# Packed copies for the dilated scores, and a paired, fixed order of the attention loop

## The chip, the cores and the metric

One core of a Trainium2 chip runs the whole block in one launch. The metric is device time in microseconds (us), the median of several executions. The engines in the profile: PE is the matrix engine (TensorE), PEld its weight loads, DVE the vector engine, ACT the scalar engine, POOL GpSimd, SP the engine whose queue issues most DMAs.

## What is computed

The reference is a transformer block on 1024 tokens of width 1024: a modulated norm, an input projection, an mLSTM mixer and a dilated attention mixer side by side, an output projection, and an expert-choice feed-forward with 16 experts. The change touches the attention mixer alone:

```python
DILATED_PATTERNS = ((128, 1), (512, 4), (2048, 16))
def dilated_attention_mixer(a_q, a_k, a_v, q_norm_g, k_norm_g, rel_bias):
    q = rms_norm(heads(a_q), q_norm_g); k = rms_norm(heads(a_k), k_norm_g); v = heads(a_v)
    outs, lses = zip(*[dilated_window_attention(q, k, v, rel_bias, w, d) for w, d in DILATED_PATTERNS])
    weights = jax.nn.softmax(jnp.stack(lses), axis=0)
    return jnp.sum(weights[..., None] * jnp.stack(outs), axis=0)
```

In a pattern with dilation d a token attends to tokens of its own phase (position modulo d) in a window. There are 8 heads of 64 columns.

## The kernel before

The kernel runs in stages: input projection and mLSTM; `phase_attn` (381 to 560 us); `phase_out`, which multiplies with the output weights and prepares the routing (560 to 680 us); and `phase_experts` (680 us to the end).

`phase_attn` works in 64 units: 4 pairs of heads, in each pair first 8 units of `order` 0 (dilation 1) and then 8 of `order` 1 (dilations 4 and 16 joined in one table), the two heads of the pair in turn. One unit is two blocks of 128 queries against 256 keys:

- `attn_A` (L807 on): for each block two score matmuls into a PSUM tile `sp` (3 buffers), with the high part `kh` (L818) and the low part `kl` (L819) of the keys; then DVE adds a table and takes the minimum (L825), and ACT takes the exponential with its sum (L830).
- `attn_B`, two units later: four transposes of `p` on PE (L845), and a copy of the result to `pT` by DVE (L855) or ACT (L857).
- `attn_C`, for two units at once: 16 matmuls with the values (L876), and a DVE copy of the result, to `ya` in order 0 (L878) or with a step of 8 floats into `O2` in order 1 (L881).

q and k lie transposed in SBUF, tokens along the row (`qT`, `kh`, `kl`, 1024 floats each). Order 0 reads neighbouring tokens. Order 1 reads them through a view: the stationary q with a step of 8 floats (`q8`), the moving keys with a step of 16 floats (`kh4`, `kl4`), quoted below.

Beside the units run side streams, one step per unit: `attn_pair_norm` (norms of the next pair of heads), `attn_pair_T` (its transposes and its split into high and low parts), `attn_load_1` and `attn_load_2` (tables and values from DRAM; `attn_load_2` loads `t_raw` into a buffer that the squares of `attn_pair_norm` use too, and ACT turns it into the order-1 table `t2`, L741), `attn_merge` (joins the outputs of the two orders of a pair; its statistics and weights go through DRAM), and `mix_stream` (L1071 to L1079). The mix stream is the mLSTM half of the output projection: 16 units of 12 matmuls, one group of 3 per step, then an ACT copy to the single buffer `mx_ev`, a POOL DMA that adds x into it, and an SP store to `part_d`, which waits for that DMA. In the loop the mix stream is asked in 7 of 8 units (`MIX = 8`); what is left of it runs in `phase_out`, together with the first steps of the merge of the last pair.

Each engine runs its instructions in a fixed sequence. Where nothing else is said, a planner chooses that sequence from the program's order and its own estimate of readiness; instructions passed to `keep_in_program_order` keep the order in which the program names them.

```python
q8 = qT.rearrange("p (n u c) -> p c u n", u=2, c=4)
kh4 = kh.rearrange("p (a b c) -> p c b a", b=4, c=4)
...
    if order == 0:
        w0 = min(max(P * i - 64, 0), S - 256)
        ql, kwh, kwl = qT[:, i * P:(i + 1) * P], kh[:, w0:w0 + 256], kl[:, w0:w0 + 256]
    else:
        ql, kwh, kwl = q8[:, i // 2, i % 2], kh4[:, i // 2], kl4[:, i // 2]
```

Of the kernel before, what the change touches and what calls it, by code (L numbers as in the profile page):

```python
# [11 lines left out]
F32 = mybir.dt.float32  # L12
F32R = mybir.dt.float32r
# [7 lines left out]
P = 128  # L21
# [30 lines left out]
MIX = 8  # L52
# [54 lines left out]
class K:  # L107
# [11 lines left out]
    def fill(self, pool, n):  # L119

        self.nc.gpsimd.memset(pool.tile([P, n // 4], F32, name="fill"), 0.0)

# [638 lines left out]

    def attn_pair_T(self, hp, psum, pool):
# [4 lines left out]
        if hp < 2:  # L767

            self.kl[hp] = []
            for z in range(2):  # L770
                kl = pool.tile([P, S], F32R, name=f"kTl{z}")
                nc.gpsimd.memset(kl[AE * (1 - z):AE * (2 - z)].bitcast(F32), 0.0)
                self.kl[hp].append(kl)
        T = [(pool.tile([P, S], F32R, name="qT", bufs=2), pool.tile([P, S], F32R, name="kTh", bufs=2), self.kl[hp % 2][z]) for z in range(2)]
        self.pairs[hp]["T"] = T
        for b in range(2):
            t = slice(b * 512, (b + 1) * 512)
            for j in (1, 0):
                pf = psum()
                for i in range(4):  # L780
                    nc.tensor.transpose(pf[:, i * P:(i + 1) * P], qk[:, j, 4 * b + i, :], self.ident)
# [18 lines left out]
    def attn_A(self, u):  # L800
# [9 lines left out]
        u["p"] = pt = [aw.tile([P, 256], F32, name="p", bufs=6) for _ in range(2)]  # L810
        for j in range(2):
            i = 2 * g + j
            if order == 0:
                w0 = min(max(P * i - 64, 0), S - 256)
                ql, kwh, kwl = qT[:, i * P:(i + 1) * P], kh[:, w0:w0 + 256], kl[:, w0:w0 + 256]
# [3 lines left out]
            nc.tensor.matmul(sp[:, j, :], ql, kwl, start=False, stop=True)  # L819
# [12 lines left out]
    def attn_B(self, u):  # L832
# [4 lines left out]
        u["ts"] = ts = aw.tile([P, 2, 2, P], F32, name="pT", bufs=3)  # L837
        for j in range(2):
            for w in range(2):
# [5 lines left out]
                nc.tensor.transpose(tp[:a1 - a0, j, w, :], pt[j][:, a0:a1], self.ident)  # L845
# [13 lines left out]
    def attn_C(self, us):  # L859
# [5 lines left out]
        for j in range(2):  # L865
            i = 2 * g + j
            for w in range(2):
                for z in range(2):
# [7 lines left out]
                    nc.tensor.matmul(op[zs, j * P:(j + 1) * P], lv, us[z]["ts"][:kp, j, w, :], start=(w == 0), stop=(w == 1))  # L876
# [58 lines left out]
    def phase_attn(self, st):  # L935
# [15 lines left out]
        for s in range(n + 3):  # L951
            if s < n:
                u = units[s]
                if s % 16 == 0:
                    self.O2[s // 16] = self.m1.tile([P, S], F32, name="O2", tag="xTh", bufs=2)
                hp = s // 16
                if s % 16 == 4 and hp:
                    self.attn_load_2(hp)
                if s % 16 == 2 and hp < 3:
                    self.attn_pair_norm(hp + 1)  # L960
                if s % 16 == 8 and hp < 3:
                    side.append(self.attn_pair_T(hp + 1, psum, aw if hp % 2 == 0 else self.ta))
                if s % 16 == 13 and hp < 2:
                    self.attn_load_qk(hp + 2)
                if s % 16 == 12 and hp < 3:
                    self.attn_load_1(hp + 1)
                self.attn_A(u)
            if s == 48:
                side.append(self.ada_rows(aw, psum, 6, 8))
            if 0 <= s - 2 < n:  # L970
                self.attn_B(units[s - 2])
            if s >= 4 and s % 2 == 0:
                self.attn_C(units[s - 4:s - 2])
            if s >= 19 and (s - 19) % 16 == 0 and s < n:
                side.append(self.attn_merge((s - 19) // 16, psum))
# [771 lines left out]
```

## Time and profile before

| | us |
|---|---|
| median of 3 executions (1836.42 to 1842.91) | 1841.47 |
| the profiled execution | 1833.95 |
| its span, first to last instruction | 1832.0 |
| input projection, mLSTM, start | 0 to 381 |
| attention loop, first to last score | 381 to 554 |
| its end and the output projection's first three rows | 554 to 594 |
| rest of the output projection, routing | 594 to 680 |
| experts | 680 to 1832 |

The time of an execution is its span and about 2 us around it. A row of a group gives line, engine, operation, output<-inputs, shape, count, then the busy time in us and the mean of one in ns, then the idle time of the engine before it. A row of a timeline gives start, duration, engine, line, operation, tiles, shape and count; durations of matmuls overlap, so a matmul's price is the distance from its start to the next start.

### The profile page before, as it was taken

What the parts mean: (1) busy time and instruction counts of PE and PEld (TensorE: products, weight loads), DVE (VectorE), ACT (ScalarE), POOL (GpSimd) and SP (SyncE); (2) the same over time, 40 slices, a digit from 0 to 9 for tenths busy, and PEclk for the clock granted to TensorE, in tenths of its full rate; (3) what the DMA queues carried; (4) which work ended last, traced back from release to release, by engine and by line L of the source; (5) the groups of instructions that cost most, each with busy time, mean ns of one, the idle gap of its engine ahead of it and who ended that gap; (6) DMA issues with size and microseconds to landing.
All of it is one profiled execution on the core that took longest, in us unless ns stands there. A gap on an engine that the chain in (4) does not pass through costs nothing. (4 is left out here: it accounts for less than half of the span.)

```text
span 1832.0 us, 24429 instructions
## 1 busy us (share of the span) xinstructions
PE 1722.9 (94%) x8696; PEld 1402.8 (77%) x8696; DVE 1487.1 (81%) x2156; ACT 1197.7 (65%) x1603; POOL 180.5 (10%) x185
## 2 busy tenths in 40 slices
PE   5999999989998939999999999999999999999997
PEld 4777888778886827888888778777787777777785
DVE  5578885687866788988988898888898888888886
ACT  5346454377763537787777777776776776777764
POOL 1001000031123020010110000100000001001000
PEclk9999999999999959999999999999999999999999
DMA  9135663325557768999999999999999999999892
GB/s 325 42 114 172 213 215 98 110 80 116 135 129 227 258 255 336 359 354 382 410 363 345 373 345 379 372 335 390 352 369 384 357 364 387 329 382 368 311 391 67
DMA packets 152553, 517.26 MB, mean 282 GB/s; under 512 B 33163, under 2 KB 50833, under 8 KB 116721
## 3 DMA queue, kind: packets, MB, share of 16 engines
q1 hardware_dynamic: 138560, 478.92, 70.7%
q0 software_dynamic: 10960, 36.32, 7.5%
q8 instruction: 68, 1.11, 0.2%
q10 hardware_dynamic: 2912, 0.48, 0.2%
q14 instruction: 53, 0.43, 0.1%
HBM read 488.16 MB, written 27.50 MB: 281 GB/s over the span
## 5 line engine op out<-in xcount | busy, mean ns | idle before, releaser
L1505 DVE TENSOR_TENSOR wl<-w,wh 128x2048 fp32r<-128x2048 f32 x278 | 627.8, 2285 | 81.6 <-ACT wh L1489 81.2
L1489 ACT ACTIVATE wh<-w 128x2048 fp32r<-128x2048 f32 x278 | 523.1, 1919 | 55.2 <-PE py L1524 26.3
L1505 DVE TENSOR_TENSOR wl<-w_half,wh 128x1024 fp32r<-128x1024 f32 x210 | 245.6, 1217 | 8.6 <-ACT wh L1489 8.5
L1489 ACT ACTIVATE wh<-w_half 128x1024 fp32r<-128x1024 f32 x210 | 211.8, 1058 | 24.1 <-PE px L1524 13.1
L1524 PE MATMUL py<-wl,xTh 128*128 128x512 f32 x512 | 139.9, 394 | 7.7 <-DVE wl L1505 7.7
L1524 PE MATMUL px<-wl,xTh 128*128 128x512 f32 x512 | 139.7, 394 | 4.5 <-DVE wl L1505 4.5
L1524 PE MATMUL px<-wh,xTh 128*128 128x512 f32 x512 | 141.1, 395 | 2.3 <-ACT xTh L124 2.1
L1524 PE MATMUL py<-wh,xTh 128*128 128x512 f32 x512 | 140.8, 394 | 2.2 <-ACT wh L1489 2.0
L1524 PE MATMUL py<-wh,xTl 128*128 128x512 f32 x512 | 138.3, 390 | 0.0
L1524 PE MATMUL px<-wh,xTl 128*128 128x512 f32 x512 | 138.1, 391 | 0.0
L1524 PE MATMUL px<-wh,hT 128*128 128x512 f32 x512 | 130.4, 396 | 0.1
L1524 PE MATMUL py<-wh,hT 128*128 128x512 f32 x512 | 129.0, 393 | 0.0
L1524 PEld LDWEIGHTS py<-wl,xTh 128*128 128x128 f32 x512 | 94.6, 188 | 33.4 <-DVE wl L1505 14.6
L1524 PEld LDWEIGHTS px<-wl,xTh 128*128 128x128 f32 x512 | 95.0, 188 | 29.5 <-DVE wl L1505 10.4
L1524 PEld LDWEIGHTS px<-wh,xTh 128*128 128x128 f32 x512 | 95.3, 189 | 23.9 <-ACT xTh L124 2.5
L1524 PEld LDWEIGHTS py<-wh,xTh 128*128 128x128 f32 x512 | 94.7, 188 | 24.0 <-ACT wh L1489 4.5
L1524 PEld LDWEIGHTS px<-wh,hT 128*128 128x128 f32 x512 | 95.6, 190 | 22.1 <-ACT wh L1489 2.1
L1524 PEld LDWEIGHTS px<-wh,xTl 128*128 128x128 f32 x512 | 96.7, 189 | 20.6
L1524 PEld LDWEIGHTS py<-wh,xTl 128*128 128x128 f32 x512 | 96.0, 188 | 20.4 <-DVE xTl L125 0.2
L1524 PEld LDWEIGHTS py<-wh,hT 128*128 128x128 f32 x512 | 95.0, 188 | 20.8 <-ACT wh L1489 0.7
L1581 POOL DMA_INDIRECT out_dram<-xin,idx x16 | 48.3, 3019 | 590.6 <-DVE xin L1580 590.6
L1445 POOL DMA_INDIRECT xin<-h_d,idx x16 | 37.8, 2362 | 477.9 <-DVE rg L1443 197.4
(456 smaller groups left out, 3138.2 us busy)
## 6 DMA issues: line engine op xcount, KB each, us to landing
w<-in_w_down_dram SPq DMA_DIRECT2D x95, 1024.0 KB, 8.4
w<-in_w_gate_dram SPq DMA_DIRECT2D x91, 1024.0 KB, 7.2
w<-in_w_up_dram SPq DMA_DIRECT2D x88, 1024.0 KB, 7.1
w_half<-in_w_gate_dram SPq DMA_DIRECT2D x70, 512.0 KB, 7.6
w_half<-in_w_up_dram SPq DMA_DIRECT2D x70, 512.0 KB, 7.5
w_half<-in_w_down_dram SPq DMA_DIRECT2D x66, 512.0 KB, 8.3
ada_w<-in_w_ada_dram SPq DMA_DIRECT2D x64, 256.0 KB, 3.5
wraw<-in_w_in_dram SPq DMA_DIRECT2D x20, 512.0 KB, 4.3
```

The costliest lines, as they stand in the source:

```text
L1445: nc.gpsimd.indirect_dma_start(out=xin, out_offset=None, in_=self.h2_d, in_offset=bass.IndirectOffsetOnAxis(ap=idx[:, :1], axis=0))
L1489: act = self.nc.scalar.activation(h[:, j * m:(j + 1) * m], t, AF.Copy)
L1505: self.tc.keep_in_program_order(self.nc.vector.tensor_sub(l[:, c], t, h[:, c]))
L1524: nc.tensor.matmul(ps[c], x[:, t], y[:, o:o + 512], start=first and q == 0 and t == 0, stop=last and (q, t) == (2, FF // N - 1))
L1581: nc.gpsimd.indirect_dma_start(out=self.out, out_offset=bass.IndirectOffsetOnAxis(ap=u["idx"][:, :1], axis=0), in_=y, in_offset=None, comp ...
```

## The change

1. `attn_turn` is new. For each pair of heads it makes six packed copies: for each head q, `kh` and `kl` in the order (phase, token in the phase), so that the tokens of a phase lie side by side. Copies 0, 3 and 5 are made by DVE, 1, 2 and 4 by ACT. They are emitted in units 1 to 6 of a pair. Order 1 then reads the copies as order 0 reads its tiles, with no step.
2. The low parts `kl` exist once, no longer in two sets, and all tiles of `attn_pair_T` come from one pool.
3. The loop goes over pairs of units: the scores of two units, two steps of the mix stream (instead of 7 in 8 units), `attn_C` for the pair three rounds back (before: two), `attn_B` for the pair one round back, then two steps of each side stream. `p` has 8 buffers instead of 6, `pT` 6 instead of 3.
4. The PE instructions of scores, transposes, values and mix stream keep the program's order (`pin`).

```diff
-MIX = 8
+    def attn_turn(self, hp, j):
+        nc, (z, what) = self.nc, divmod(j, 3)
+        src = self.pairs[hp]["T"][z][what]
+        dst = self.aw.tile([P, S], F32R, name=("qP", "kPh", f"kPl{z}")[what], bufs=1 if what == 2 else 2)
+        if what == 0:
+            o, i = dst.rearrange("p (c u n) -> p c u n", c=4, u=2), src.rearrange("p (n u c) -> p c u n", u=2, c=4)
+        else:
+            o, i = dst.rearrange("p (c b a) -> p c b a", c=4, b=4), src.rearrange("p (a b c) -> p c b a", b=4, c=4)
+        if j in (0, 3, 5):
+            nc.vector.tensor_copy(o, i)
+        else:
+            nc.scalar.activation(o, i, AF.Copy)
+        self.pairs[hp].setdefault("turned", []).append(dst)
...
-        T = [(pool.tile([P, S], F32R, name="qT", bufs=2), pool.tile([P, S], F32R, name="kTh", bufs=2), self.kl[hp % 2][z]) for z in range(2)]
+        T = [(pool.tile([P, S], F32R, name="qT", bufs=2), pool.tile([P, S], F32R, name="kTh", bufs=2), self.kl[z]) for z in range(2)]
...
-        qT, kh, kl = pr["T"][h % 2]
-        q8 = qT.rearrange("p (n u c) -> p c u n", u=2, c=4)
-        kh4 = kh.rearrange("p (a b c) -> p c b a", b=4, c=4)
-        kl4 = kl.rearrange("p (a b c) -> p c b a", b=4, c=4)
+        qT, kh, kl = pr["turned"][3 * (h % 2):][:3] if order else pr["T"][h % 2]
...
-                ql, kwh, kwl = q8[:, i // 2, i % 2], kh4[:, i // 2], kl4[:, i // 2]
-            nc.tensor.matmul(sp[:, j, :], ql, kwh, start=True, stop=False)
+                w0 = i // 2 * 256
+            ql, kwh, kwl = qT[:, i * P:(i + 1) * P], kh[:, w0:w0 + 256], kl[:, w0:w0 + 256]
+            self.pin(nc.tensor.matmul(sp[:, j, :], ql, kwh, start=True, stop=False))
...
+        for s2 in range(0, n + 6, 2):
+            for s in (s2, s2 + 1):
+                if s < n:
...
+                        side.append(self.attn_pair_T(hp + 1, psum, self.ta))
+                    if 1 <= s % 16 <= 6:
+                        self.attn_turn(hp, s % 16 - 1)
...
+                    self.attn_A(u)
...
+            for _ in range(2):
+                done = next(self.mix, True)
+            if 0 <= s2 - 6 < n:
+                self.attn_C(units[s2 - 6:s2 - 4])
+            if 0 <= s2 - 2 < n:
+                for u in units[s2 - 2:s2]:
+                    self.attn_B(u)
+            for x in side * 2:
                 try:
                     next(x)
                 except StopIteration:
-                    side.remove(x)
-            if s % MIX != MIX - 1:
-                done = next(self.mix, True)
+                    if x in side:
+                        side.remove(x)
```

## Rows read from the trace of the kernel before

**Rows 1.** The page's first line: the profiled span.

```profile
span 1832.0 us, 24429 instructions
```

**Rows 2.** Stretches: length, busy time (instructions) of each engine, PE clock, DMA.

```profile
core 0: us, PE busy (x) PEld busy (x) DVE busy (x) ACT busy (x) POOL busy (x), PEclk, DMA share, GB/s
381.00:395.00 14.00, 13.80 (x107) 11.65 (x108) 13.69 (x44) 13.97 (x36) 5.01 (x4) 1.00 0.16 56
381.00:553.50 172.50, 170.05 (x1219) 141.56 (x1220) 135.26 (x436) 129.90 (x379) 37.71 (x31) 1.00 0.50 116
...
680.00:1832.00 1152.00, 1118.08 (x5104) 906.35 (x5102) 995.77 (x738) 836.44 (x764) 82.94 (x31) 0.99 0.93 352
```

**Rows 3.** Waits, 381 to 553.5 us: who for whom, us, times, longest.

```profile
ACT p L830 <- DVE stats L825: 15.1, 19, 1.9
...
DVE p L825 <- PE sp L819: 9.5, 12, 1.5
```

**Rows 4.** Groups by shape, 381 to 595 us: busy us, mean ns, idle before.

```profile
L818 PE MATMUL sp<-kTh,qT 128*128 128x256 f32 x128 | 47.0, 377 | 3.5 <-ACT ev L426 3.5
...
L881 DVE COPY O<-op 128x256 f32<-128x256 f32 x16 | 10.6, 661 | 6.5 <-PE op L876 6.4
...
L124 ACT ACTIVATE wmh<-wo_raw 128x512 fp32r<-128x512 f32 x12 | 7.4, 629 | 6.1 <-POOL wo_raw L1167 2.7 <-PE mx L1073 2.0 <-DVE wo_raw L1167 1.3
...
L878 DVE COPY ya<-op 128x256 f32<-128x256 f32 x16 | 6.7, 421 | 7.3 <-PE op L876 7.3
...
L125 DVE TENSOR_TENSOR yal<-ya,mix 128x1024 fp32r<-128x1024 f32 x4 | 4.9, 1219 | 0.1
...
L124 ACT ACTIVATE ogh<-og 128x1024 fp32r<-128x1024 f32 x4 | 4.2, 1058 | 0.0
...
L1029 DVE COPY col_b<-mod_cols 128x512 f32<-128x512 f32 x2 | 0.8, 424 | 0.0
```

**Rows 5.** PE timeline, order 0: four scores, four transposes, three mix matmuls.

```profile
473.56 0.28 PE L818 MATMUL sp<-kTh,qT 128*128 128x256 f32 x1
...
474.03 0.60 PE L845 MATMUL tp<-ident,p 128*64 128x128 f32 x4
474.39 0.48 PE L1071 MATMUL mx<-wmh,ogh 128*128 128x512 f32 x1
474.70 0.40 PE L1072 MATMUL mx<-wml,ogh 128*128 128x512 f32 x1
474.93 0.40 PE L1073 MATMUL mx<-wmh,ogl 128*128 128x512 f32 x1
```

**Rows 6.** PE timeline, order 1: the second row starts eight scores later.

```profile
453.22 0.42 PE L819 MATMUL sp<-kTl,qT 128*128 128x256 f32 x1
...
455.19 0.29 PE L845 MATMUL tp<-ident,p 128*128 128x128 f32 x1
```

**Rows 7.** PE timeline: a group of value matmuls between two mix matmuls.

```profile
471.55 0.48 PE L1071 MATMUL mx<-wmh,ogh 128*128 128x512 f32 x1
471.96 1.09 PE L876 MATMUL op<-pT,vs 128*64 128x128 f32 x16
472.98 0.50 PE L1072 MATMUL mx<-wml,ogh 128*128 128x512 f32 x1
```

**Rows 8.** ACT and DVE timelines: next norms' square, the order-1 table, its first use.

```profile
466.39 1.06 ACT L753 ACTIVATE qk_sq<-qk 128x1024 f32<-128x1024 f32 x1
...
488.27 1.06 ACT L741 ACTIVATE t<-t_raw 128x1024 f32<-128x1024 f32 x1 [0.39 <-DMA t_raw<-tab_d]
...
489.36 0.42 DVE L825 CUSTOM_DVE_ANT_0 p<-sp,t 128x256 f32<-128x256 f32 x1 [1.21 <-ACT t L741]
```

**Rows 9.** DVE and SP timelines, `phase_out`: merge weights, their store, x loads.

```profile
566.28 0.28 DVE L917 COPY mw<-pm 32x128 f32<-32x128 f32 x1 [0.45 <-PE pm L915]
...
569.82 0.42 SPq L919 DMA_DIRECT2D w_d<-mw  x1
...
581.30 3.75 SPq L1191 DMA_DIRECT2D xres<-part_d  x7
```

More of the change, by code (lines that the diff above doesn't have):

```diff
@@ L780, in attn_pair_T @@
                 for i in range(4):
[L781 removed]
+                    self.pin(nc.tensor.transpose(pf[:, i * P:(i + 1) * P], qk[:, j, 4 * b + i, :], self.ident))
                 for z in range(2):
@@ L844, in attn_B @@
                     a1 = P + 64
-                nc.tensor.transpose(tp[:a1 - a0, j, w, :], pt[j][:, a0:a1], self.ident)
+                self.pin(nc.tensor.transpose(tp[:a1 - a0, j, w, :], pt[j][:, a0:a1], self.ident))
         A = slice(0, P)
@@ L875, in attn_C @@
                         lv = pair["vs"][:, i // 2, w, zs]
-                    nc.tensor.matmul(op[zs, j * P:(j + 1) * P], lv, us[z]["ts"][:kp, j, w, :], start=(w == 0), stop=(w == 1))
+                    self.pin(nc.tensor.matmul(op[zs, j * P:(j + 1) * P], lv, us[z]["ts"][:kp, j, w, :], start=(w == 0), stop=(w == 1)))
         if order == 0:
@@ L950, in phase_attn @@
         side = []
[L951 to L975, printed above, removed]
-            for x in list(side):
@@ new lines, in phase_attn @@
+        for s2 in range(0, n + 6, 2):
+            for s in (s2, s2 + 1):
+                if s < n:
+                    u = units[s]
+                    if s % 16 == 0:
+                        self.O2[s // 16] = self.m1.tile([P, S], F32, name="O2", tag="xTh", bufs=2)
+                    hp = s // 16
+                    if s % 16 == 4 and hp:
+                        self.attn_load_2(hp)
+                    if s % 16 == 2 and hp < 3:
+                        self.attn_pair_norm(hp + 1)
+                    if s % 16 == 8 and hp < 3:
+                        side.append(self.attn_pair_T(hp + 1, psum, self.ta))
+                    if 1 <= s % 16 <= 6:
+                        self.attn_turn(hp, s % 16 - 1)
+                    if s % 16 == 13 and hp < 2:
+                        self.attn_load_qk(hp + 2)
+                    if s % 16 == 12 and hp < 3:
+                        self.attn_load_1(hp + 1)
+                    self.attn_A(u)
+                if s == 48:
+                    side.append(self.ada_rows(aw, psum, 6, 8))
+                if s >= 19 and (s - 19) % 16 == 0 and s < n:
+                    side.append(self.attn_merge((s - 19) // 16, psum))
+            for _ in range(2):
[6 more added lines that the diff above has]
+            for x in side * 2:
@@ L1070, in mix_stream @@
                     (h, l), (wh, wl) = hs[k], W[k]
-                    nc.tensor.matmul(ps, h[:, t], wh, start=(k == 0), stop=False)
-                    nc.tensor.matmul(ps, h[:, t], wl, start=False, stop=False)
-                    nc.tensor.matmul(ps, l[:, t], wh, start=False, stop=(k == MH - 1))
+                    self.pin(nc.tensor.matmul(ps, h[:, t], wh, start=(k == 0), stop=False))
+                    self.pin(nc.tensor.matmul(ps, h[:, t], wl, start=False, stop=False))
+                    self.pin(nc.tensor.matmul(ps, l[:, t], wh, start=False, stop=(k == MH - 1)))
                     if k < MH - 1:
```

15 lines of the change are left out of this document (8 added, 7 removed).

## The prediction

> **What bounds the kernel now.** I read the page first: the span is 1832.0 us [rows 1]. Then the stretches. The change edits the attention loop, 381 to 553.5 us, so the question is what ends last there. PE is shown busy for 170.05 of 172.5 us, DVE for 135.26, ACT for 129.90 [rows 2]; PE's clock is granted in full. The waits agree: ACT waits for DVE's table step (15.1 us) and DVE for PE's scores (9.5 us) [rows 3], so the queue starts at PE. The reader should distrust "170 busy" all the same, since matmul durations overlap; what a matmul costs is the distance to the next start, and those distances are where the change acts.
>
> In order 0 four scores take 474.03 - 473.56 = 0.47 us, 0.118 each [rows 5]. In order 1, the same tiles read with a step, eight scores take 455.19 - 453.22 = 1.97 us, 0.246 each [rows 6]. Four transposes take 0.36 us, and the mix matmul behind them 0.31 instead of 0.23 (474.39, 474.70, 474.93) [rows 5]: 0.44 for a set. Sixteen value matmuls take 1.02 us, and the mix matmul ahead of them 0.41 instead of 0.23 [rows 5, 7]: 1.20 for a group.
>
> What is won in this stretch stays won: the experts are a stretch of their own with PE busy for 1118 of 1152 us [rows 2], and they start when the stages before them have ended.
>
> **The change, part by part.**
>
> *Packed reads on PE.* 128 blocks with two scores each (L818 has 128) [rows 4] are 256 scores, half of them order 1. 128 x (0.246 - 0.118) = 16.4 us leave PE. This has one answer, since order 0 reads the same element types at 0.118.
>
> *PE's whole need.* To the last score: 256 scores x 0.118 = 30.2; 64 sets of transposes x 0.44 = 28.2; 29 value groups x 1.20 = 34.8; mix matmuls: 64 calls, 4 of which go to the gate rows, so 60 x 3 x 0.23 = 41.4; some 83 transposes and small matmuls of the side streams at 0.36 for four, 7.5. Sum 142. The same sum for the kernel before (order 1 at 0.246, and 52 x 3 mix matmuls, 7 calls in 8 less 4) is 46.6 + 28.2 + 34.8 + 35.9 + 7.5 = 153 of 172.5: some 19 us of breaks, groups cut in two and switches between kinds. The pairs and the fixed order should remove part of them. PE's need after is 142 us without breaks and 161 with as many as before. So PE stops being the only bound, whatever else happens.
>
> *The copies.* 24 of 128x1024 floats, 12 on DVE, 12 on ACT. No row shows a strided read on either. DVE: a packed SBUF copy of 512 floats takes 424 ns [rows 4], so two of them, 0.85 us, are the low end; a two-input operation at one float a step takes 1.22 us [rows 4]; and the strided write of L881 costs (661 - 421) / 256 = 0.94 ns per float more than the packed one of L878 [rows 4], which would make it 1.22 + 0.96 = 2.18. I take 1.22: the row nearest to a strided read is PE's own, 0.246 us for 256 columns, 0.96 ns per element [rows 6], less than the 1219 / 1024 = 1.19 that DVE takes per float anyway. 12 x 1.22 = 14.6 us, ends 10.2 and 26.2. ACT: packed 1058 ns, and 629 for 512 [rows 4], so 0.84 ns per float; at 0.96 it is 1.18 us, at the double 1.92. 12 x 1.18 = 14.2 us, ends 12.7 and 23.0.
>
> [...]
>
> *DVE and ACT after.* DVE 135.3 + 14.6 = 149.9 us (ends 145.5 and 161.5), ACT 129.9 + 14.2 = 144.1. DVE becomes the engine with the most to do. How full can it get? In the first 14 us, where the mix stream's operands are split, DVE is busy for 13.69 and ACT for 13.97 [rows 2]: 98%. At 98% DVE needs 153.0 us.
>
> *The wait that comes next.* The order-1 table hangs on the norms of the next pair, since they share a buffer: square at 466.39, then two reductions on DVE, eight loads, ACT's reversal at 488.27, first use at 489.36, where DVE waited 1.21 us for it [rows 8]. That is 22.97 us for about eight units, with no slack left. At 153.0 / 64 = 2.39 us per unit eight units last 19.1; 3.9 us are missing, in two of the four pairs (the first has its table early, and beside the last no norms run). DVE's copies are even queued ahead of the reductions. I add 2 x 3.9 = 7.7; ends 0 and, with a DVE queue longer by three copies of 2.18, 2 x 10. The stretch is then 153.0 + 7.7 = 160.7 instead of 172.5: -11.8 us.
>
> *Deeper buffers, one set of `kl`.* Order-1 scores read copies, so `kl` is free once order 0 and the last copy of unit 6 are done, before the next pair is written from unit 8 on. I cost it at nothing; if that cover fails, a split waits some tenths of a us, three times.
>
> *The mix stream.* All of it now fits in the loop (192 matmuls instead of 168): 24 x 0.23 = 5.5 us move out of `phase_out`, with two ACT copies, two POOL DMAs and two SP stores. SP gets to wait for the POOL DMA more often in less time; behind it stand the loads of the next pair, which is inside the 7.7 above. After the loop the merge of the last pair is the chain: its weights were ready on DVE at 566.28 + 0.28 and their store went out at 569.82, because SP stood behind a mix store [rows 9]. These 3.3 us go. Against it, the eight x loads, which followed the last mix store (581.30, 3.75 us of issue) [rows 9], can now go ahead of that store. Ends -5.5 (PE's own part, should the merge not matter) and +4 (the x loads ahead). I take -3.3.
>
> **Sum.** -11.8 - 3.3 = -15.1 us. The profiled execution took 1833.95 us, 2 more than its span, and would come to 1818.9; it lies below all three timed runs, so against the median of 1841.47 the forecast is 1826.4. Half a per cent, about what a measurement of this kernel can tell from no change, is 9.2 us here.
>
> **The rivals.**
>
> 1. *DVE fills and nothing waits for the table.* Copies between 0.85 and 1.22 us (148 to 153 us at 98%), stretch near 150: -22.5 - 3.3, which gives 1815.7. For it: the planner starts norms early where it can. Against: the table's slack was nil before.
> 2. *The copies cost their upper ends.* DVE 161.5 / 0.98 = 164.8, plus 7.7, is 172.5, just the old length; with -3.3 it comes to 1838. For it: L881's price for a step. Against: L881 steps on the write, and these copies write packed. [...]
> 3. *The fixed order makes PE wait (slower).* Between the last score of a round and its first transpose PE has 6 mix matmuls, a value group, 8 transposes, 8 scores, 6 mix matmuls and a value group: 1.4 + 1.2 + 0.9 + 0.9 + 1.4 + 1.2 = 7.0 us. ACT works 144.1 / 32 = 4.5 us per round on average, more where splits or norms of the next pair fall in. Once it is over 7.0 us late, PE stands at the transposes, and the next scores and mix matmuls, which the planner could have put ahead, stand behind them; so DVE and ACT then starve too. From 0.47 us lost per round (15.1 / 32) the change wins nothing; at 1.0 it is -15.1 + 32 = +16.9 us, 1858. For it: three engines within 8 us of each other, and in-order queues. Against: two rounds of slack and deeper `p` and `pT`.
> 4. *The change doesn't do what it says:* order 1 stays at 0.246 for another reason than the step, and only the copies remain. Order 0 speaks against it. PE then needs 158 to 177: about 1845.
>
> **How the numbers follow.** Forecast 0.45, by itself 1818 to 1835 (DVE's copy price and the table's wait); rival 1 0.16; rival 2 0.22; rival 3 0.14; rival 4 0.03. Faster by over 0.5% means under 1832.3: three quarters and more of the forecast (0.37), all of rival 1, a little of rival 2: 0.54. Slower, over 1850.7: the greater part of rival 3 and nothing else, 0.11. Same: 0.35. The range leaves out the lower half of rival 1 and most of rival 3: 1814 to 1845.
>
> **What would show it.** Right: order-1 scores at 0.12 us from start to start; DVE busy for over 90% of the stretch from first to last score, which lasts about 161 us; copies near 1.2 us on both engines; the first order-1 table step of pairs 1 and 2 waiting some us for ACT's reversal; `w_d` out less than 1 us after its weights. Wrong: copies of 2 us; PE idle ahead of L845 with ACT as releaser in most rounds; a chain in `phase_out` longer than before; or PE still without gaps, at more than 142 us for the loop, which would say that the breaks, not the step, were its price.

## The result, and the profile after

The changed kernel takes 1858.8 us (median of 4 runs, 1856.3 to 1860.6) beside 1840.1 for the kernel before (4 runs): a ratio of 1.0102, interval 1.0079 to 1.0125. It is slower by 18.7 us; the forecast was 1826.4, faster by 15. The page of the profiled execution begins:

```profile
span 1857.2 us, 24429 instructions
```

That is 25.2 us more than in [rows 1], where the medians differ by 18.7: the profiled execution of the kernel before lies 6 us under its median, that of the changed kernel at its own. To see where the time went, I took the same stretches as in [rows 2], then cut both kernels at the same events: first score, last score, first transpose of the output rows (which needs the last merge and the whole output product of its rows). Stretches of the kernel after; columns are length, busy us (instructions) of each engine, granted PE clock, DMA share, GB/s:

```profile
core 0: us, PE busy (x) PEld busy (x) DVE busy (x) ACT busy (x) POOL busy (x), PEclk, DMA share, GB/s
381.00:395.00 14.00, 8.16 (x48) 7.75 (x48) 12.49 (x32) 10.95 (x24) 4.82 (x5) 0.76 0.18 60
381.00:553.50 172.50, 144.63 (x1114) 116.88 (x1115) 138.61 (x418) 144.04 (x365) 39.61 (x32) 0.93 0.48 115
680.00:1832.00 1152.00, 1109.85 (x5083) 899.40 (x5084) 1008.27 (x817) 841.70 (x772) 88.68 (x42) 0.99 0.94 355
...
383.50:563.60 180.10, 154.71 (x1200) 125.37 (x1201) 143.32 (x442) 149.91 (x386) 39.21 (x31) 0.93 0.48 114
563.60:622.80 59.20, 37.65 (x200) 28.60 (x199) 26.21 (x50) 15.71 (x32) 18.79 (x38) 0.80 0.72 224
```

And the last two stretches in the kernel before:

```profile
381.20:553.40 172.20, 169.95 (x1219) 141.45 (x1219) 135.23 (x436) 129.60 (x378) 37.55 (x31) 1.00 0.50 116
553.40:594.30 40.90, 35.42 (x177) 27.17 (x177) 24.08 (x43) 15.05 (x30) 15.14 (x39) 0.96 0.82 237
```

I call the first of them the loop and the second the tail. The loop took 180.1 us instead of 172.2, the tail 59.2 instead of 40.9; the loop began 2.3 us later, and what follows the tail took 3.3 us less: 7.9 + 18.3 + 2.3 - 3.3 = 25.2. So the larger loss lies behind the code that was rewritten. In the loop PE is no longer busy throughout (154.71 of 180.1), as the packed reads promised, and yet nobody else is full: DVE 80%, ACT 83%.

The reads did what they should. PE's timeline in order 1, start, us, engine, line (the scores are 0.12 us apart; 0.246 in [rows 6]):

```profile
423.96 0.28 PE L834 MATMUL sp<-kPl,qP 128*128 128x256 f32 x1
424.08 0.28 PE L833 MATMUL sp<-kPh,qP 128*128 128x256 f32 x1
```

The copies, grouped by shape (busy us, mean ns): ACT takes 2.0 us for one, DVE 1.1 to 1.4.

```profile
L777 ACT ACTIVATE kPh<-kTh 128x1024 fp32r<-128x1024 f32 x8 | 16.1, 2014 | 0.0
L775 DVE CAST qP<-qT 128x1024 fp32r<-128x1024 f32 x8 | 9.1, 1134 | 0.0
L777 ACT ACTIVATE kPl<-kTl 128x1024 fp32r<-128x1024 f32 x4 | 8.1, 2026 | 0.0
L775 DVE CAST kPl<-kTl 128x1024 fp32r<-128x1024 f32 x4 | 5.7, 1419 | 0.0
```

PE's waits from 381 to 625 us (who waited for whom: us, times, longest):

```profile
PE pm L1204 <- ACT mix L127: 16.4, 2, 10.3
PE mx L1092 <- ACT ogh L127: 6.8, 1, 6.8
PE mx L1092 <- ACT mx_ev L1098: 6.2, 6, 2.0
PE tp L799 <- ACT pT L872: 4.8, 5, 2.6
PE mx L1093 <- DVE wml L128: 4.0, 1, 4.0
```

The first line is the tail: two standstills at the output product (L1204), of 6.1 and 10.3 us. The others are the loop (but for one of the six waits for `mx_ev`, 2.0 us at 569), mostly at mix matmuls that stand in PE's fixed order ahead of scores.

What stands behind those 10.3 us is one chain through the last merge, here from the timelines of DVE, PE, SP and ACT (an entry in brackets is idle time before it and its releaser):

```profile
584.87 0.18 DVE L927 TENSOR_TENSOR me<-me,ml 128x16 f32<-128x16 f32 x1
...
599.99 0.27 PE L930 MATMUL pm<-ident,me 128*32 128x128 f32 x1
...
600.61 0.32 SPq L934 DMA_DIRECT2D w_d<-mw  x1
...
609.70 1.23 DVE L945 TENSOR_TENSOR ya<-ya,wb 128x1024 f32<-128x1024 f32 x1 [9.12 <-DMA wb<-w_d]
614.34 1.23 DVE L947 TENSOR_TENSOR ya<-ya,wb 128x1024 f32<-128x1024 f32 x1 [3.42 <-POOL wb L944]
...
615.60 1.06 ACT L127 ACTIVATE mix<-ya 128x1024 fp32r<-128x1024 f32 x1 [16.15 <-DVE ya L947]
...
616.71 0.80 PE L1204 MATMUL pm<-wmh,mix 128*128 128x512 f32 x1 [10.30 <-ACT mix L127]
```

The merge's weights were ready for their transpose at 584.87 + 0.18. It ran at 599.99, 15 us later, and PE was not waiting for it: it worked through output-product matmuls that stood ahead of it in its queue. The kernel before ran this transpose 12.6 us behind the last score, as soon as its operand was there:

```profile
565.97 0.27 PE L915 MATMUL pm<-ident,me 128*32 128x128 f32 x1 [2.33 <-DVE me L912]
```

The kernel after ran it 36.4 us behind the last score. The cause is in the code of `phase_out`: the merge's steps are issued one for each mix step that is left over (`for _ in self.mix: next(merge, 1)`). Before, of 4 + 64 steps 59 were asked for in the loop and one more finished a tile, so 8 were left, and they drove the merge past its transpose (its seventh step) and the store and loads of its weights. Now 70 are asked and none is left. The merge's steps then come from the output product alone, one behind every second group of its matmuls (`if n % 2: next(merge, 1)`), so that the transpose stands in PE's queue behind the products of the first three rows with the first two of the four `mix` tiles.

### The profile page after: what moved, and what is told of

The parts are those of the page before. It is cut to its first block, busy times and chain, and to the rows that moved or that the text cites. A ratio compares the mean times of both kernels' runs of the same rounds, so it can differ in the third digit from the quotient of the medians.

```text
span 1857.2 us, 24429 instructions
## 1 busy us (share of the span) xinstructions
PE 1709.4 (92%) x8696; PEld 1387.7 (75%) x8696; DVE 1498.0 (81%) x2168; ACT 1218.7 (66%) x1615; POOL 183.2 (10%) x183
## 5 line engine op out<-in xcount | busy, mean ns | idle before, releaser
L1545 PEld LDWEIGHTS px<-wh,xTh 128*128 128x128 f32 x512 | 95.3, 189 | 23.8 <-ACT xTh L127 2.5
```

The lines of the kernel that those rows point to most:

```text
L1545: nc.tensor.matmul(ps[c], x[:, t], y[:, o:o + 512], start=first and q == 0 and t == 0, stop=last and (q, t) == (2, FF // N - 1))
```

## The experiments

Two stories could explain the loss: the loop (copies dearer than foreseen, or the fixed order), or the tail (the requests of the mix). The runs take the change apart in both directions; each has its label in brackets. Times are medians, ratios are to runs of the kernel before on the same chip, with their 95% interval; loop and tail are those of the profiled execution. On the chips of the experiments the kernel before took 1835.7 to 1837.9, not 1840.1, so kernels are compared by the ratios and not by the times.

| kernel | time, us | ratio | loop | tail |
|---|---|---|---|---|
| before (profiled span 1832.0) | 1840.1 | 1 | 172.2 | 40.9 |
| after | 1858.8 | 1.0102 (1.0079 to 1.0125) | 180.1 | 59.2 |
| before + copies (e1) | 1837.9 | 1.0019 (1.0006 to 1.0031) | 177.3 | 42.3 |
| before + packed reads of other tokens, no copies (e8) | 1826.6 | 0.9936 (0.9914 to 0.9958) | 160.9 | 46.3 |
| before + copies that don't reorder, at half price (e13) | 1836.4 | 1.0005 (0.9993 to 1.0017) | 174.9 | 42.3 |
| before + copies, all on DVE (e7) | 1847.1 | 1.0055 (1.0038 to 1.0071) | 182.4 | 46.2 |
| before + copies, all on POOL (e9) | 1853.8 | 1.0099 (1.0083 to 1.0116) | 191.2 | 43.3 |
| before + copies of keys only (e10) | 1847.4 | 1.0059 (1.0038 to 1.0080) | 185.4 | 44.6 |
| before + copies of queries only, DVE (e16) | 1842.1 | 1.0034 (1.0021 to 1.0047) | 182.1 | 43.9 |
| before + copies of queries only, POOL (e18) | 1841.0 | 1.0028 (1.0018 to 1.0039) | 175.8 | 41.7 |
| before + requests (e21) | 1847.6 | 1.0060 (1.0043 to 1.0076) | 178.3 | 49.5 |
| before + spaced splits (e20) | 1853.9 | 1.0093 (1.0075 to 1.0110) | 178.8 | 55.6 |
| after - copies (e2) | 1857.1 | 1.0123 (1.0106 to 1.0140) | 176.4 | 55.9 |
| after - copies, packed reads of other tokens (e15) | 1848.3 | 1.0059 (1.0040 to 1.0078) | 175.8 | 59.1 |
| after - fixed order (e3) | 1851.4 | 1.0085 (1.0068 to 1.0102) | 178.6 | 55.3 |
| after - requests (e4) | 1864.6 | 1.0166 (1.0149 to 1.0183) | 196.0 | 45.4 |
| after - requests - fixed order (e17) | 1841.0 | 1.0016 (1.0004 to 1.0028) | 170.6 | 44.2 |
| e17 + spaced splits (e19) | 1840.3 | 1.0022 (1.0012 to 1.0031) | 169.2 | 50.4 |
| after + merge early (e5) | 1842.1 | 1.0034 (1.0020 to 1.0048) | 181.2 | 44.1 |
| e5 - fixed order (e14) | 1843.8 | 1.0037 (1.0023 to 1.0052) | 177.9 | 49.8 |

A single execution of one kernel can lie some us from its median (e17: 1834.0 to 1844.4), so the loop and tail columns carry an uncertainty of a few us that the ratios don't. The profiled executions of e2, e4 and e17 lie 4 to 7 us under their medians, those of e10, e15 and e16 5 to 6 us over them.

### The tail

**e5, the merge early.**

```diff
             for _ in self.mix:
                 next(merge, 1)
+            for _ in range(7):
+                next(merge, 1)
             for k in range(MH):
```

> The changed kernel with seven steps of the last merge taken before the output product's matmuls are issued, as the mix steps left over after the loop drove them in the kernel before; everything else, the mix requests among it, is the changed kernel's. Theory tail, its form with the merge: from last score to first transpose of the output rows 41 to 48 us instead of 59, time 1842 to 1849, the statistics' transpose of the last merge at 6 to 10 us behind the last score instead of 36. Rival, the tail's other form (the last mix evictions hold ScalarE and the store of `part_d` holds the merge's store): the stretch stays over 54 us, time 1854 or more.

The tail fell from 59.2 to 44.1 us and the time to 1842.1. In PE's timeline the transpose now waits for its operand, as a step on the chain should, 18.2 us behind the last score (6 to 10 were expected):

```profile
580.45 0.37 PE L930 MATMUL pm<-ident,me 128*32 128x128 f32 x1 [6.38 <-DVE me L927]
```

With nothing else altered, two thirds of the change's loss are gone (0.34% instead of 1.02%). The rival, that the last mix evictions hold the tail by themselves, falls.

**e21, the requests alone**, in the kernel before:

```diff
-            if s % MIX != MIX - 1:
-                done = next(self.mix, True)
+            done = next(self.mix, True)
```

> The kernel before with one part of the change, its smallest: a mix step asked for in every unit instead of 7 in 8, so that the mix is used up when the loop ends (8 steps, two tiles, fewer behind it). No copies, no pairs, no fixed order. Theory requests (the change's largest loss is this one): the loop takes 5 to 8 us more, 177 to 181, the stretch behind it goes from 40.9 to 54 to 60 us, as the steps of the last merge are no longer driven by mix steps there, time 1852 to 1860, as slow as the whole change. Rival (the loss needs the copies or the pairs too): within 5 us of the kernel before.

One line makes the kernel before slower by 0.60%, 11 us. Loop +6.1, tail +8.6, the merge's transpose 26.9 us behind the last score and the same standstill behind it as in the kernel after. From PE's waits in the tail, and its timeline:

```profile
PE pm L1182 <- ACT mix L124: 10.7, 2, 10.3
...
589.26 0.27 PE L915 MATMUL pm<-ident,me 128*32 128x128 f32 x1
```

The time is below the 1852 that was expected: the requests carry some 60% of the loss by themselves (0.60 of 1.02%), and the tail is 10 us shorter than the changed kernel's. What the changed kernel has besides is a mix eviction that waited 6.82 us on ACT for a store and held the operand splits of the output product behind it:

```profile
580.11 0.60 ACT L1098 ACTIVATE mx_ev<-mx 128x512 f32<-128x512 f32 x1 [6.82 <-DMA part_d<-mx_ev]
```

That is the standstill of 6.1 us. By the traces PE stands there for 5.8 us in e2, which has no copies, and for 5.2 in e3, which has no fixed order, so neither of these is needed for it; e4 and e17, where the requests are taken out, don't show it.

**e4 and e17, the requests taken out of the changed kernel**, with the fixed order (e4) and without it (e17; there `pin` keeps nothing in order):

```diff
-            for _ in range(2):
-                done = next(self.mix, True)
+            for s in (s2, s2 + 1):
+                if s % 8 != 7 and s < n + 3:
+                    done = next(self.mix, True)
```

> The changed kernel with the mix asked for in 7 of 8 units, as in the kernel before, so that the last mix steps stay for the stretch after the loop and drive the last merge there. Theory tail: the stretch from last score to first transpose of the output rows falls from 59 us to 41 to 47 us, the loop stays within 3 us of 180 us, time 1841 to 1848. Theory order: the last evictions of the mix block ScalarE whatever drives the merge, the stretch stays over 52 us and the time at 1852 or more.

> The changed kernel with the mix asked for in 7 of 8 units and without the fixed order, so that only the copies, the pairs of units and the deeper buffers are left of the change. With the fixed order and these requests the loop was 196.0 us, nine standstills of 20.9 us in all among them, each at a mix matmul behind the eviction of the mix tile before it. Theory fixed order (these standstills are the order's, since the same requests put the next tile's first matmul straight behind the eviction): without it the loop falls to 172 to 180 us, the stretch behind it stays at 45 us, time 1838 to 1846. Rival (the standstills belong to the requests, whatever the order): the loop stays over 186 us.

The tail came back as foreseen, 45.4 and 44.2 us. But e4's loop grew to 196.0 us, which neither theory had (its time, 1864.6, lies in the range of theory order, but through the loop and not through the tail), and e17 explains it. PE's waits in the loop, e4, then e17:

```profile
PE mx L1093 <- ACT mx_ev L1099: 20.9, 9, 5.0
```

```profile
PE mx L1093 <- ACT mx_ev L1099: 3.1, 5, 1.6
```

The mix has one PSUM tile. With two steps a round, as the change asks, a tile of four steps ends with a round, and the next tile's first matmul comes a round behind the eviction. Skipping one step in eight shifts that: the first matmul follows the eviction at once, and in a fixed order PE stands there, 2.3 us each of nine times. Without the fixed order the planner fills the gap, and the loop is 170.6 us. So the fixed order was worth 25 us of loop with one set of requests and 1.5 with the other (below).

### The fixed order

**e3, the changed kernel without it:**

```diff
     def pin(self, ins):
-        self.tc.keep_in_program_order(ins)
+        return ins
```

> The changed kernel with the fixed order taken out: the same instructions, copies, pairs and mix requests, and TensorE's instructions go where the planner puts them. Theory tail: the stretch after the last score stays at 57 to 61 us, since the mix is still used up in the loop. Theory order: the loop falls from 180 us to 160 to 170 us, as the standstills at mix matmuls go, time 1840 to 1850. Theory copies: the loop stays within 3 us of 180 us, time 1855 to 1862.

Loop 178.6 instead of 180.1, time 1851.4: the theory that the order costs the loop 10 us and more falls. By the ratios it costs 0.17%, 3 us, but the two intervals overlap, so that it costs anything with these requests isn't shown. **e14** adds the early merge to this:

> The changed kernel with both cures at once: the last merge's seven steps ahead of the output product's matmuls, and no fixed order. If the two causes are separate, the loop is that of the changed kernel without fixed order (178.6 us) and the stretch behind it that of the changed kernel with the early merge (44.1 us), time 1838 to 1842. If the fixed order is what held the first stretch of the merge, less than 1836.

1843.8, two us over what was expected: the early merge, but without the order, left a tail of 49.8 (the transpose ran 24.0 us behind the last score, not 18.2). The two cures don't add. By DVE's timelines the merge waited for its statistics to come back from DRAM: the first step that needs them ran 19.0 us behind the last score in e14, 14.9 in e5 (their load took 6.1 us from issue to that step instead of 2.7), and from there to the transpose DVE did three splits of the output product between the merge's steps instead of two (5.0 us instead of 3.3). Why the load took longer stays open.

### The copies

**e8, the reads without copies, and e1, with them:**

```diff
-                ql, kwh, kwl = q8[:, i // 2, i % 2], kh4[:, i // 2], kl4[:, i // 2]
+                ql, kwh, kwl = qT[:, i * P:(i + 1) * P], kh[:, i // 2 * 256:i // 2 * 256 + 256], kl[:, i // 2 * 256:i // 2 * 256 + 256]
```

> The kernel before with one edit: order 1 reads its queries and keys side by side, straight from the transposed tiles, and no copies are made (so these scores take the tokens of order 0's neighbourhoods; the same instructions, sizes and waits otherwise). It is the gain of the reads by itself. Theory TensorE's need (the loop is bound by TensorE): the loop falls from 172 us by 12 to 16 us, to 156 to 160, time 1820 to 1824. Rival (the loop is bound by the chain through the evicting engines; TensorE only fills the breaks): the loop falls by less than 6 us, to 166 us or more, time 1830 or more.

> This kernel has the copies and the packed order-1 reads of the change, and the loop, the order of the steps, the buffers and the mix requests of the kernel before. Reference points, profiled: kernel before, loop (first score to last score) 172.2 us, from last score to the first transpose of the output rows 40.9 us; changed kernel 180.1 and 59.2. Theory tail (the mix is used up inside the loop, so nothing drives the last merge after it): the tail is as before, 41 us, and the time is within 10 us of the kernel before. Theory order (the fixed order of TensorE costs the loop, the copies alone gain): the loop is 158 to 168 us and the time 1826 to 1836. Theory copies (the copies on ScalarE at 2.0 us each, 24 us in all, make the loop's two evicting engines late): the loop is 176 us or more here too and the time 1844 or more.

(In e8 order 1 reads order 0's neighbourhoods, so its scores are of other tokens; e13 and e15 below do the same. e1 has `attn_turn`, one set of `kl` and the packed reads of the change in the loop of the kernel before.) Stretches from first to last score, e8, then e1:

```profile
381.60:542.50 160.90, 155.99 (x1219) 126.20 (x1220) 133.76 (x431) 127.98 (x373) 37.95 (x31) 0.99 0.51 124
```

```profile
383.20:560.60 177.40, 164.17 (x1219) 129.38 (x1220) 147.25 (x448) 150.47 (x390) 36.30 (x30) 0.97 0.47 112
```

The reads alone take 11.3 us from the loop and 0.64% from the time: PE was the bound. The copies give back 16.5 us of loop (0.9936 to 1.0019, 15 us of time). e1's loop is the one of theory copies; its time, 1837.9, and its tail, 42.3, are those of theory tail. In e1 DVE is busy for 83% and ACT for 85% of the loop: neither fills, and PE's need has fallen too. That the engines wait for each other in turn is how I read it; no run shows it by itself.

**e13, the same copies without the reordering, and so cheaper:**

```diff
-        if what == 0:
-            o, i = dst.rearrange("p (c u n) -> p c u n", c=4, u=2), src.rearrange("p (n u c) -> p c u n", u=2, c=4)
-        else:
-            o, i = dst.rearrange("p (c b a) -> p c b a", c=4, b=4), src.rearrange("p (a b c) -> p c b a", b=4, c=4)
+        o, i = dst, src
```

> The copies alone in the kernel before's loop, with the same 24 copies on the same engines, but each copies its tile straight through, so that no copy reads strided and order 1 gets the tokens in order 0's sequence. The copies on ScalarE then take 1.06 to 1.18 us, the prediction's price, instead of 2.01, some 10 us of ScalarE less. Theory price (the prediction failed in the size of the copies): the loop falls from 177.3 us to 160 to 166. Theory ceiling (it failed in letting the evicting engines be busy 98 percent: with 160.9 us for the reads alone there is no room for even the smaller copies): the loop is 170 us or more.

The groups by shape:

```profile
L775 ACT ACTIVATE kPh<-kTh 128x1024 fp32r<-128x1024 f32 x8 | 8.4, 1051 | 0.0
L773 DVE CAST qP<-qT 128x1024 fp32r<-128x1024 f32 x8 | 5.6, 705 | 0.0
```

At 52% of ACT's price and 62% of DVE's the loop is still 174.9 us: 2.4 us less than e1, of 16. The theory of the price falls. The number of the theory of the ceiling holds: DVE was busy 139.5 us of that loop, 80%, and no run of this study got DVE over 87% (e7) or ACT over 88% (e19). But a fixed share isn't the limit either: e8 ran DVE at 83% in a loop 14.0 us shorter. What e13's loop has besides is a slower PE; its granted clock has a mean of 0.95, against 0.99 in e8 and 1.00 in the kernel before:

```profile
382.30:557.20 174.90, 165.67 (x1218) 131.66 (x1219) 139.54 (x448) 139.79 (x389) 36.93 (x30) 0.95 0.47 113
```

In steps of 1 us, PE's busy time multiplied by what the clock lacks of 1 adds up to 8.1 us in e13's loop, 4.3 in e1's, 1.7 in e8's and none in that of the kernel before: an estimate of the work that PE didn't get done. So 6.4 of the 14.0 us go with the clock, and 4.3 more are idle time of PE. What makes PE stand in the first place, no run separates.

**e7 and e9, all copies on one engine** (the condition in `attn_turn` sends all 24 to DVE, or to POOL):

> The kernel before with the copies and the packed reads alone (its own loop and order), all 24 copies on VectorE instead of 12 on each engine. With 12 on each, the loop is 177.3 us. Theory copies on ScalarE (2.0 us each, in front of the mix splits and the moves of the probabilities, are what takes back the gain): the loop is 160 to 172 us, time 1822 to 1834. Theory VectorE (an engine with 138 us of work in the loop gets 13 us more and is the bound): the loop is 177 to 186 us, time 1838 to 1848. Theory TensorE's need (the loop was bound by TensorE, as the prediction had it): 158 to 166 us wherever the copies are.

> The kernel before with the copies and the packed reads alone, all 24 copies on GpSimd, which is busy in 43 of 189 us around the loop. No run here has such a copy on GpSimd; its multiply of 128x1024 in the last merge took 2.3 us. Theory copies (what takes back the gain is the time of the copies on the two evicting engines): at 2 to 3 us a copy GpSimd has 50 to 70 us more and still room, the loop is 158 to 168 us, time 1822 to 1832. Rival (a copy takes 4 us or more there, or order 1 waits for it): the loop is 177 us or more.

On DVE the loop is 182.4 us: the theory that only ACT's price hurts falls, and the numbers of theory VectorE hold. On POOL it is worse, 191.2, though a copy took 2.2 to 2.3 us as expected: POOL's queue also holds the mix evictions' DMAs and the merge's multiply, and one copy waited 12.4 us for PE to release its target, with all of these behind it.

**e10, e16, e18, half the operands.** e10 copies the keys only, e16 the queries only (DVE), e18 the queries only (POOL):

> The copies alone in the kernel before's loop (loop 177.3 us with 24 copies), with the 8 copies of the queries left out: order 1 reads its queries strided, as weights of TensorE, and its copied keys side by side, as moving columns. Two questions. Which operand costs the 0.13 us a strided score has: if the moving columns, order-1 scores start 0.118 us apart as with all copies, if the weights 0.24. What a copy costs the loop: at the mean of all 24 (177.3 minus 160.9 with reads alone = 16.4 us, 0.68 us a copy) eight less give 172 us and 1832 to 1834; theory single engine (VectorE, which made these eight, is not what is late): 175 us or more, 1836 or more.

> The kernel before with the copies of the queries alone: 8 copies, 1.13 us each on VectorE, order 1 reads its weights side by side and its keys, the moving columns, strided as before; loop, order, buffers and key tiles are before's. With the queries strided and the keys copied, order-1 scores started 0.205 to 0.226 us apart, 0.246 with both strided, 0.118 with neither. Theory weights (nearly all of the strided cost is the weight load's): order-1 scores start 0.12 to 0.15 apart, 8 copies cost the loop some 4 us of the 11 that the reads give, the loop is 164 to 169 us instead of 172, time 1828 to 1833. Rival (each operand strided sets the same pace): order-1 scores still start over 0.2 apart, the loop is 174 us or more, time 1837 or more.

> The same as the kernel with the queries' copies alone, with these 8 copies on GpSimd instead of VectorE, at 2.0 to 2.9 us each. If the evicting engines' time is what a copy costs, the loop is 161 to 165 us and the time 1826 to 1830; if GpSimd's place in the mix (its multiplies and its DMA issues wait behind a copy) costs as much, 167 us or more.

PE's timelines in order 1, strided queries (e10), then strided keys (e16):

```profile
456.25 0.41 PE L839 MATMUL sp<-kPh,qT 128*128 128x256 f32 x1
456.49 0.41 PE L840 MATMUL sp<-kPl,qT 128*128 128x256 f32 x1
```

```profile
452.61 0.40 PE L839 MATMUL sp<-kTl,qP 128*128 128x256 f32 x1
452.83 0.40 PE L838 MATMUL sp<-kTh,qP 128*128 128x256 f32 x1
```

0.24 us with the weights strided, 0.22 with the moving columns strided, 0.246 with both, 0.118 with neither: each operand sets the pace by itself, and half the copies buy nothing: all three kernels are slower than the kernel before. (The 0.205 to 0.226 us that e16's expectation gives for e10 was misread.) The rival of e16 held: to win the reads all three tiles have to be copied. e10's loop, 185.4, falls in the open range of its second theory, but not for that theory's reason: its scores were at 0.24 us again while 16 copies stayed. e18's loop is its second case. e16 also prices copies where little is won back: its 8 took 10.2 us on DVE (1.27 each), and the time rose by 0.34%, 6 us.

### The pairs

**e2 and e15, the new order without copies**, with strided reads (e2) and with packed ones (e15):

> This kernel has the rounds in pairs of units, the fixed order, the deeper buffers and the mix requests of the change, but no copies: order 1 reads the strided tokens as the kernel before does, with its two pairs of correction tiles. Theory tail: from last score to first transpose of the output rows 57 to 61 us, as in the changed kernel. Theory order: the loop is as long as in the changed kernel or longer by up to the 16.4 us of the strided reads (180 to 197 us), time 1859 to 1876. Theory copies: without them the loop falls to 172 us or less, and the time to 1851 or less.

> The changed kernel's order (pairs, fixed order, buffers, mix requests) with order 1 reading side by side straight from the transposed tiles and no copies, so that these scores take the tokens of order 0's neighbourhoods. It is the fourth corner: no copies and before's loop 160.9 us, copies and before's loop 177.3, copies and the new order 180.1. Theory additive (the order costs the loop some 4 us by itself, as its 176.4 against 172.2 with strided reads says): 164 to 168 us here, and with a tail of 56 us a time of 1843 to 1849. Theory fixed order hides the gain (TensorE stands in its order for others whatever it has to do): 172 us or more, 1851 or more.

e2's tail, 55.9, is the long one of the requests, as theory tail had it; its loop, 176.4, is shorter than theory order had it. e15's loop is 175.8, the second theory's number, while its time is the first one's. The medians decide: 1857.1 and 1848.3, by the ratios 1.0123 and 1.0059, so the packed reads bring 0.64% in this order too, just what they bring in the order of before (e8). The profiled loops differ by 0.6 us only, but they don't compare: e2's is its fastest execution, 1850.4, and e15's its slowest, 1854.1. So the theory that the fixed order hides the gain isn't borne out.

**e19 and e20, the splits of the mix spaced.** Near 400 us ACT and DVE split four mix operands in one block, and the four units there took 23.8 us in e17, 15.9 in e8. e19 puts one split to a unit in e17, e20 does the same in the kernel before, each asking for a mix step in every unit:

```diff
                     raws.append(self.w_half(k, 1))
+                if k < MH - 1:
+                    yield False
```

> The changed kernel without the fixed order, with 7 mix steps left for the stretch after the loop, and with the operand splits of the mix spaced: one of the four weight and value splits to a unit instead of all four in one step (six more steps in all, and one asked in every unit). With all four in one step, ScalarE and VectorE ran 10 us of splits on end near 400 us with no score's work between (23.8 us for 4 units there, where the reads alone took 15.9). Theory congestion (the copies cost where they meet the splits): the loop falls from 170.6 to 160 to 166 us, time 1828 to 1835 beside 1841. Rival (the splits only move): 168 us or more, 1838 or more.

> The kernel before with the splits of the mix spaced in the same way and a mix step asked in every unit, nothing of the change in it: the control of the run beside it. Its loop is bound by TensorE, which is busy in 170 of 172 us by the profile: if that holds, the loop stays within 3 us of 172 and the time within 4 us of the kernel before; if the block of splits holds up TensorE here too, 165 us or less, 1828 to 1832.

e19's four units fell to 11.3 us and the next four rose from 7.0 to 17.7: the work only moved, as the rival said (and 4 steps were left for the tail, not the 7 of the expectation). e20 missed both expectations for a reason of its own: with the six steps more, the loop's last tile takes the mix to 4 steps left instead of 8 (74 steps, 67 asked, 3 to finish the tile), the merge's transpose comes 29.8 us behind the last score, and the tail is 55.6. PE ran 36 mix matmuls behind the last score there, as many as in the kernel before. So it isn't PE's work in the tail that counts but how many steps issue the merge: 8 left gave tails of 41 to 46 us, 4 left 50 and 56, none left 50 to 59, and none left with the merge issued by hand 44 (50 without the fixed order).

### The sum

Along one path from the kernel before to the kernel after, by ratios: copies and reads (e1) +0.19% (reads -0.64, copies +0.83); pairs and deeper buffers (e17 against e1) -0.03; requests (e3 against e17) +0.69; fixed order (after against e3) +0.17. Together 1.02%: 3.5 - 0.6 + 12.7 + 3.1 = 18.7 us. The intervals of e1 and e17 overlap, and so do those of e3 and the kernel after, so the second and the fourth step aren't clear of noise; the reads, the copies and the requests are. The steps of another path differ: requests alone 0.60; or pairs, order and requests without copies +1.23 (e2), reads -0.64 (e15), copies +0.43 (after). No kernel here beats the kernel before with the same scores; the nearest is e17 at +0.16%. Only e8 is faster, and it leaves the copies out, so that its scores are of other tokens.

## Why the prediction was wrong

*What bounds the kernel.* Right: PE. Taking 16.4 us from PE took 11.3 us from the loop (e8). The reads' price was exact, 0.12 us from start to start.

*"After the loop the merge of the last pair is the chain", with 3.3 us to win.* The chain was right, the sign wrong, and this is the step that decided: -3.3 us forecast for the tail, +18.3 measured (e21, e5 and e17 against e3 show the requests as the cause). I looked at what the mix steps cost in `phase_out` (PE time, stores in SP's way) and not at what they did there, which was to issue the merge. The sign that I named as right came true and meant nothing: `w_d` went out 0.03 us behind its weights (600.30 + 0.28, then 600.61) instead of 3.26 [rows 9], but 31 us later in the program. That the deferred x loads or the freed stores counted, no run shows.

*"At 98% DVE needs 153.0 us."* Wrong, the second large step. The 98% came from 14 us in which the splits of the mix lay ready in a row [rows 2]. A loop in which each unit passes PE, DVE, ACT, PE, DVE or ACT, and PE again didn't do that here: the most that DVE reached in any run is 87%. The kernel before ran DVE at 78% beside a full PE [rows 2]. The loop was forecast at 160.7, which is what the reads give with no copies at all; with the copies it measured 177.3 (e1), and 174.9 with copies under the predicted price (e13). At 85%, the predicted 149.9 us of DVE would give 176 us, but that share is chosen after the fact. The sum also had no term for a PE that runs at a lower clock, by the estimate above 6.4 of e13's 14.0 us. What sets the loop with the copies in it stays open.

*The copies.* DVE's 1.22 us was near (1.13; 1.42 for `kPl`), ACT's 1.18 too low: 2.01, over the upper end of 1.92. With a step in the read each engine took longer than without: 2014 against 1051 ns for a copy on ACT, 1134 against 705 on DVE (the change against e13), and 0.22 to 0.246 against 0.118 us for a score on PE (e16, e10 and the kernel before against order 0). But the size mattered little: e13 got 2.4 us back.

*The wait for the table.* 7.7 us were added for DVE's first order-1 step waiting for ACT's table. None of DVE's waits in the changed loop has that releaser (the kernel before had one, 1.2 us [rows 8]). ACT did idle ahead of the table, for 6.4 us in two waits for its loads, from ACT's waits in the loop:

```profile
ACT t L744 <- DMA t_raw<-tab_d: 6.4, 2, 5.1
```

That the two numbers are near is luck.

*The mix in the loop.* I counted 5.5 us out of the tail, and nothing into the loop, since DVE was to be the bound there. The requests alone lengthened the loop by 6.1 (e21).

*The rivals.* The slower outcome had a rival, the fixed order, at 0.47 us a round from which nothing would be won. It cost 1.5 us of the profiled loop, 0.05 a round and not clear of noise, and the waits that I named (transposes behind ACT) are 1.2 us in two places; PE stood at mix matmuls instead. As a mechanism it is real, as e4 shows (2.3 us a standstill). Rival 2 came nearest for e1, 1838 and 1837.9, but it laid that to the price of the copies, and e13 shows that the price was little of it.

## What to carry to other kernels

Before work is moved out of a stage, read what else it does there: a loop that steps one stream may be what issues another, and here the stage that had lost its drivers was slower although less was done in it (e21's tail took 49.5 us instead of 40.9). The high busy share of a short stretch (98% of 14 us) gave no ceiling for this loop, which goes back and forth between engines; take it from a run of the loop (here DVE was busy for 73 to 87%). A gain on the bound is worth measuring without its price first (e8): it showed in one run that 11 us were to be had and that any way of paying for it had to stay under that. And before two loops are compared by their profiles, see where each profiled execution lies among its kernel's times: e2 and e15 look alike by profile and differ by 9 us.

## What the runs showed of the hardware

PE's granted clock fell in the standstills of 6.8 and 6.1 us. The changed kernel's two windows near 400 us (columns as above):

```profile
391.00:401.00 10.00, 3.19 (x24) 2.99 (x24) 5.95 (x19) 10.00 (x24) 2.32 (x3) 0.84 0.00 0
401.00:411.00 10.00, 9.87 (x45) 6.99 (x45) 10.00 (x15) 5.76 (x11) 6.12 (x4) 0.62 0.33 106
```

In 6.8 us of idling for `ogh` (393.9 to 400.7) the granted clock fell from 1.00 (392 to 398 us) to 0.50 (399 to 408 us), which gives the mean of 0.62 in the second window; the kernel before had 1.00 over the whole loop, the changed kernel 0.93. In the tail it shows in the matmuls themselves: 0.43 us apart behind the standstill of 6.14, at a clock of 0.50 (583 to 592 us), 0.23 later on, at 1.00 (593 to 610 us).

```profile
583.52 0.80 PE L1204 MATMUL pm<-woh,mix 128*128 128x512 f32 x1 [6.14 <-ACT mix L127]
584.11 0.63 PE L1205 MATMUL pm<-wol,mix 128*128 128x512 f32 x1
584.54 0.63 PE L1204 MATMUL pm<-woh,mix 128*128 128x512 f32 x1
...
600.33 0.39 PE L1205 MATMUL pm<-wml,mix 128*128 128x512 f32 x1
600.56 0.40 PE L1206 MATMUL pm<-wmh,yal 128*128 128x512 f32 x1
```

So these two standstills were paid twice, as idle time and as slower matmuls behind them.

A read with a step of 64 bytes about doubled ACT's time for a copy (1051 to 2014 ns), one of 32 added 60% to DVE's (705 to 1134), and a score on PE took about twice as long (0.118 to 0.246 us); on PE it was enough that one of the two operands was strided (0.22 and 0.24).
